# Expert weights of the second block read in rows of 1024 columns instead of halves of 512

## The chip, the cores and the metric

The kernel runs on one core of one Trainium2 chip. The metric is the device time of one execution in microseconds. It is the time of the whole kernel, two transformer blocks on 256 tokens of 1024 features, of which the change touches the mixture of experts in the second block.

## The reference

Everything is fp32. The second block has two layers; after each layer's mixer (a state-space mixer in layer 0, attention in layer 1) stands a mixture of 16 experts in which each expert picks its 32 best tokens of a sample. In layer 0 it runs on two samples, the latent tokens x and the context tokens; in layer 1 on x alone. All three matrices of an expert are 1024 x 1024:

```python
def moe_ec(h, router_w, w1, w3, w2):
    """Expert choice: each expert picks its top-C tokens of this sample's routed set."""
    b, T, _ = h.shape
    cap = EC_CAPACITY * T // N_EXPERTS_2
    logits = jnp.einsum('btd,de->bte', h, router_w, preferred_element_type=jnp.float32)
    aff = jax.nn.softmax(logits, axis=-1)
    gate, idx = lax.top_k(jnp.swapaxes(aff, 1, 2), cap)
    bidx = jnp.arange(b)[:, None, None]
    xg = h[bidx, idx]
    a = jnp.einsum('becd,edf->becf', xg, w1)
    g = jnp.einsum('becd,edf->becf', xg, w3)
    y = jnp.einsum('becf,efd->becd', jax.nn.silu(a) * g, w2)
    y = y * gate[..., None].astype(y.dtype)
    return jnp.zeros_like(h).at[bidx, idx].add(y.astype(h.dtype))
```

The result is the final rmsnorm of x after layer 1. The experts' weights are 2 x 16 x 3 matrices of 4.19 MB, 402.7 MB of the 597 MB that the kernel reads.

## The kernel before

The first block (mixer, attention over a memory, grouped experts) takes the first part of the time and isn't touched. In the second block, `choice` sets up a layer's experts, `choice_route` chooses the tokens and builds `xg`, the chosen rows turned to features (128 features on the partitions, 8 chunks k), and `choice_run` runs the experts in groups that fill 128 rows: layer 0 has 64 rows per expert (two samples of 32), so EG = 2 experts in each of 8 groups; layer 1 has 32 rows, so EG = 4 in each of 4 groups.

`choice_group` does one group. `product` (matmul at L1773) multiplies the group's rows with a matrix: the rows of expert j use their own S = 64 or 32 columns of TensorE (`tile_position=(0, j * S)`), so the experts of a group can run beside each other; the output is one PSUM bank, 128 x 512. For each half n of the hidden columns: w1's half into one bank, w3's half into another, tanh on ACT (L1804), two DVE operations that make silu(a) * g (L1805, L1806), four transposes on PE (L1809), a copy on ACT into `actT` (L1810). Then, for each half n of w2's columns: the product, scaled into `y` as a high and a low part (ACT L1815, DVE L1816); per sample and per 128 tokens two matmuls that put the rows back to their tokens (L1822), a product with the gate row on DVE (L1825) and the addition to x or ctx (L1826, on DVE for the first 128 tokens, on POOL for the others).

The weights come through a ring of slots of 16 KB per partition (`ring`, L110), 2.097 MB each: seven slots in layer 0 (the last opens when the routing's own pool closes), nine in layer 1. `choice_tile` (L1635) fills a slot by EG DMAs, one per expert, from SP's queue: the q-th part of the rows of EG experts, half n of the columns, that is 8 / EG chunks of 128 rows x 512 columns, so 2 KB of consecutive memory per row. Each layer has 96 such tiles. A slot is loaded again when PE has read its tile for the last time.

A scheduler sets the order of each engine's instructions from a simulated time; PE's first products of layer 0 and layer 1 stand among the last steps of the routing (L1741), which builds `xg` chunk by chunk. The final norm's gain row is loaded into `ctx_x[:, 0]`, the context's tile, which is free in layer 1 and serves as `actT` there (L2072 to L2075).

Of the kernel before, what the change touches and what calls it, by code (L numbers as in the profile page):

```python
# [22 lines left out]
AF = mybir.ActivationFunctionType  # L23
OP = mybir.AluOpType
AX = mybir.AxisListType
PSUM = bass.MemoryType.PSUM
DRAM = bass.MemoryType.DRAM

P = 128
# [49 lines left out]
class Net:  # L79
# [16 lines left out]
    @contextmanager  # L96
    def psum(self, **bufs):
        """PSUM's eight banks by the tags that a phase takes them under"""
        self.n += 1
        with self.tc.tile_pool(name=f"psum{self.n}", bufs=1, space=PSUM, reuse_waits="tile") as p:  # L100
            old = self.pp, self.pb
            self.pp, self.pb = p, bufs
            yield
            self.pp, self.pb = old
# [5 lines left out]
    def ring(self):  # L110
        """the next weight slot: the lasting ring and a phase's own in turn"""
# [7 lines left out]
        if hold is not None:  # L119
            # its load is not to come before what the phase at hand loads  # L120
            self.nc.gpsimd.tensor_copy(t[:, :1], hold)
# [3 lines left out]
    def weight_slots(self, n, side=None):  # L125
        """n more slots for weights, used in turn with those there are"""
# [38 lines left out]
    def columns(self, groups):  # L165
        """vectors over features, turned into one value per partition"""
# [31 lines left out]
    def load_more(self):  # L198
# [4 lines left out]
        # vectors laid out in every partition  # L203
# [25 lines left out]
    def rstd(self, ss, n, width):  # L229
        """(ss / width + EPS) ** -0.5 for [P, n]"""  # L230
# [16 lines left out]
    def norm_rows(self, xs, A4, rs=None):  # L247
        """rows scaled to unit mean square (no gain): one tile per 128 rows"""
# [13 lines left out]
    def norm_halves(self, xs, tile_, rs=None):  # L262
        """the same in tiles of 128 rows' halves; row tile i's chunk k"""
# [19 lines left out]
    def to_features(self, rows, g, hT, t0=0):  # L283
        """hT[:, k, t0:] = gain * transposed rows"""
# [17 lines left out]
    def rope(self, o, x, cg, sg, tmp, twice=None):  # L302
        """o = x * cg + swapped halves of x * sg; [P, 2, heads, d] with tables [P, 2, d]"""
# [14 lines left out]
    def twice(self, o, x, y, op):  # L318
        """o [P, 2, heads, 2, d]: x op y, twice"""
# [4 lines left out]
    def head_rms(self, x, sq, width):  # L324
        """x [P, 2, heads, width] scaled by its heads' rstd; sq a scratch of its shape"""
# [37 lines left out]
    def gained(self, g, d0, d, step, name):  # L363
        """tables of rope with the gain g of its dims in it"""
# [29 lines left out]
    def attend(self, PT, L, v_of, o_ps, shared):  # L394
        """o_ps [P = (parity, 64), heads / 2, P] from weights L [P, heads, nk]"""
# [70 lines left out]
    def chunks(self, *tiles):  # L466
        """of (hi, lo) tiles the list of their chunks' pairs"""
        return [(hi[:, k], lo[:, k]) for hi, lo in tiles for k in range(hi.shape[1])]

    def to_features_split(self, rows, g, hT):  # L470
        """gain * transposed rows, as a pair of which the sum is that"""
# [13 lines left out]
    def wpairs(self, how, pieces, K, c):  # L485
        """a weight in pairs of its K chunks of 128 rows: [P, 2, c] each"""
# [14 lines left out]
    def split_w(self, how, w):  # L501
        """a pair of a weight's chunks, split: for each chunk its hi and lo"""
# [10 lines left out]
    def lin3(self, how, w, hT):  # L513
        """rows of h times w: one PSUM tile per 128 rows"""
# [9 lines left out]
    def feat3(self, how, w, hT, done):  # L524
        """w^T h, feature-major, two chunks of 128 outputs per PSUM tile: done(chunk, psum)"""
# [11 lines left out]
    def mixer(self, keep, tile_, pool):  # L537
# [23 lines left out]
        # indexer  # L561
# [11 lines left out]
        # latent projections  # L573
# [8 lines left out]
        # queries of the attention over the chosen keys  # L582
# [56 lines left out]
        # gates: tanh of half the logits  # L639
# [8 lines left out]
        # the merge, feature-major: 2 * merged  # L648
# [37 lines left out]
    def index_mask(self, i, s):  # L686
        """0 for the 64 highest scores among the keys that a query sees, NEG for the others"""
# [9 lines left out]
    def latent_heads(self, h0, cT, kpe, tile_, M):  # L697
        """queries, keys (turned) and values of four heads"""
# [66 lines left out]
    def padded_keys(self, tile_, k, cT, sT, tag):  # L765
        """one key head, turned: kT[:, 0] has it in partitions 0:64, kT[:, 1] in 64:128"""
# [14 lines left out]
    def pairs_T(self, A4, q):  # L781
        """[P, 2, 2n heads, 64] -> [P = (parity, 64), n, T]"""
# [13 lines left out]
    def memory_keys(self, keep, M, G):  # L796
        """two pieces of work that wait for nothing: the memory's keys (turned) and values"""
# [43 lines left out]
    def memory_read(self, keep, pool):  # L841
# [3 lines left out]
        # queries, feature-major; the norm's gain is in their weights, its rstd with their own in the logits  # L845
# [76 lines left out]
    def raw_features(self, x, junk, put):  # L922
        """both 128 rows of x, turned: put(where, psum); the rstd of their norm"""
# [15 lines left out]
    CAP = 64  # L939

    def group_moe(self, pool, tile_, late):
# [20 lines left out]
        # group: softmax, first of the largest  # L962
# [19 lines left out]
        # experts of the group: the two largest of affinity + bias  # L982
# [22 lines left out]
        # place of a token in its expert's queue  # L1005
# [5 lines left out]
        # 1000 for a token that isn't there  # L1011
# [15 lines left out]
        # the context's rows will be normalised next  # L1027
# [9 lines left out]
    def group_weights(self, what):  # L1037
        """of a pair of experts half of the rows of gate and up, or all of down"""
# [15 lines left out]
    def down_half(self, late, pr, n):  # L1054
        """half of the columns of a pair of experts' down"""
# [6 lines left out]
    def group_round(self, r, ahead, tile_, late, hi, lo, pos, comb):  # L1062
        """tokens whose place in their expert's queue is in CAP * r + [0, CAP)"""
# [33 lines left out]
        for pr in range(E // 2):  # L1097
            if pr == 2:
                gather(1, "tf")
            # where the slots come from, and their weights  # L1100
# [81 lines left out]
    def ada_step(self, l, n=1):  # L1182
        """n 48ths of layer l's modulation: each from 128 of the features a sixth of its columns"""
# [51 lines left out]
    def mod_cols(self, l, which, r):  # L1235
        """per feature: norm_w * (1 + scale), shift"""
# [7 lines left out]
    def to_features_mod(self, rows, m, sh, hT, t0, tmp=None):  # L1244
        """hT[:, k, t0:] = m * transposed rows + sh; with tmp, hT is a pair of which the sum is that"""
# [22 lines left out]
    def split(self, hi, lo, x, eng=None):  # L1268
        """x = hi + lo, each in float32r"""
# [3 lines left out]
    def mm3(self, p, L, R, start, stop, **kw):  # L1273
        """p += L^T R of split operands (all but the product of the two small parts)"""
# [42 lines left out]
    def ssd_steps(self, tile_, tmp_, A4, hT):  # L1317
        """step sizes and the cumulative sums of the decays; directions and heads over the partitions"""
# [41 lines left out]
        # from here on each of a direction's heads in four of the partitions  # L1360
# [10 lines left out]
        for d in range(2):  # L1371
# [11 lines left out]
            # moving side: cumulative sums of a quarter of the heads  # L1383
# [13 lines left out]
            # stationary side  # L1397
# [13 lines left out]
            # weights of the context's tokens in the state it leaves  # L1411
# [10 lines left out]
            # sums from x's first (or last) token on  # L1422
# [13 lines left out]
    def ssd_project(self, g, pt_, xt_, hT):  # L1436
        """a group's four heads, B and C, all convolved, and the gate; feature-major"""
# [59 lines left out]
    def ssd_group(self, g, xs, BT, CT, zz, tile_, last=None):  # L1497
# [22 lines left out]
        for q in range(2):  # L1520
# [7 lines left out]
            for st in range(2):  # L1528
                M = tile_([P, 4, T], "M", 2)
                ex = []  # L1530
                # (direction, stationary variant, tile of the rows l, on the diagonal)
# [19 lines left out]
        # the context's final states, and what they give x's tokens  # L1551
# [37 lines left out]
    def ssd_out(self, q, tile_):  # L1589
        """the context's tokens (q = 0) or x's"""  # L1590
# [32 lines left out]
    def ssd_rstd(self):  # L1623
        """of the gated rows, from their squares' sums by partition"""
# [10 lines left out]
    def choice_tile(self, nm, l, e0, EG, q, n):  # L1635
        """the q-th part of EG experts' rows, half n of their columns: [P, EG, 8 / EG, 512]"""
        K = 8 // EG
        v = self.ring().rearrange("p (e k c) -> p e k c", e=EG, k=K)
        for e in range(EG):
            src = self.a[nm][l, e0 + e, q * K * P:(q + 1) * K * P, n * 512:(n + 1) * 512]  # L1640
# [3 lines left out]
    def choice(self, l, samples, pool):  # L1644
        """samples: (token rows, row of the modulation); what of the experts' work lasts"""
# [462 lines left out]
```

## Time and profile before

| | us |
|---|---|
| median of 3 runs | 2299.51 (2298.75 to 2302.57) |
| the profiled execution's span | 2296.6 |
| outside the span | 2.9 |
| PE busy | 1981.3 (86%) |
| DVE, ACT, POOL busy | 966.7, 637.2, 449.2 |
| share of the chain that is `DMA w<-in_moe_w_dram` | 21% of the span |
| HBM read | 597.05 MB, 262 GB/s over the span |

All times below are from one profiled execution, and they stand against its own span of 2296.6 us; the other 2.9 us of the median lie outside of it. A line such as L1773 is a line of the kernel; names of tiles are given without their numbers, so `w` is any weight tile and `ps` any PSUM bank. A share of the DMA engines near or over 1 means that all 16 have packets all the time.

### The profile page before, as it was taken

How to read it: one execution, taken by the hardware profiler on the slowest of the kernel's cores; microseconds unless marked ns; L12 is line 12 of the kernel's file. 1: busy time of each engine (PE TensorE's matmuls, PEld its weight loads, DVE VectorE, ACT ScalarE, POOL GpSimd, SP SyncE). 2: the span in 40 equal slices, each digit the busy share in tenths (PEclk: the TensorE clock that was granted, in tenths of full speed). 3: DMA queues.
4: the chain of work that ended last, by engine and by line, in shares of the span. 5: the costliest groups of instructions: out<-in, count | busy, mean ns of one | idle time of the engine just before them, and what ended most of it. 6: DMA issues, size and time to landing. Idle time of an engine off the chain costs nothing. (4 is left out here: it accounts for less than half of the span.)

```text
span 2296.6 us, 24819 instructions
## 1 busy us (share of the span) xinstructions
PE 1981.3 (86%) x9384; PEld 1019.8 (44%) x9384; DVE 966.7 (42%) x1675; ACT 637.2 (28%) x1174; POOL 449.2 (20%) x487
## 2 busy tenths in 40 slices
PE   8889878889999999898898888887988788888886
PEld 7667633366776677565332222222755311111111
DVE  6875532268776677665312222223675210100101
ACT  6454422254554455443100000002453000000000
POOL 4430110032242232511101011112652000000000
PEclk9999989989999999999999999999999799999999
DMA  7554849823332322474999999998349899999997
GB/s 235 186 189 142 286 143 346 287 79 111 120 117 95 110 83 84 150 245 174 363 386 387 386 386 387 387 387 331 149 165 329 299 386 387 386 387 387 387 387 280
DMA packets 339421, 603.53 MB, mean 263 GB/s; under 512 B 23611, under 2 KB 97118, under 8 KB 339294
## 3 DMA queue, kind: packets, MB, share of 16 engines
q1 hardware_dynamic: 339294, 601.86, 73.7%
q8 instruction: 76, 1.25, 0.2%
q14 instruction: 51, 0.42, 0.1%
HBM read 597.05 MB, written 4.75 MB: 262 GB/s over the span
## 5 line engine op out<-in xcount | busy, mean ns | idle before, releaser
L1773 PE MATMUL ps<-w,xg 128*64 128x512 f32 (+1 forms) x2048 | 506.1, 611 | 95.2 <-DMA w<-in_moe_w_dram 95.1
L1773 PEld LDWEIGHTS ps<-w,xg 128*64 128x64 f32 (+1 forms) x2048 | 128.1, 124 | 445.6 <-DMA w<-in_moe_w_dram 267.3
L1826 POOL TENSOR_TENSOR x<-x,o 128x512 f32<-128x512 f32 x24 | 39.2, 1635 | 695.1 <-DVE o L1825 695.1
L1276 PE MATMUL ps<-hT,ws 128*128 128x512 f32 x384 | 162.3, 423 | 4.1 <-DVE ada L1215 4.1
L1773 PE MATMUL ps<-w,ctx 128*32 128x512 f32 x512 | 139.5, 608 | 25.6 <-DMA w<-in_moe_w_dram 25.6
L1278 PE MATMUL ps<-hT,ws 128*128 128x512 f32 x384 | 156.1, 406 | 0.0
L1277 PE MATMUL ps<-hT,ws 128*128 128x512 f32 x384 | 155.8, 406 | 0.0
L1773 PE MATMUL ps<-w,actT 128*64 128x512 f32 x512 | 126.7, 599 | 10.7 <-DMA w<-in_moe_w_dram 9.8
L1805 DVE SCALAR_TENSOR_TENSOR act<-act,ps 128x512 f32<-128x512 f32 x24 | 16.5, 687 | 252.6 <-ACT act L1804 252.6
L1806 DVE TENSOR_TENSOR act<-act,ps 128x512 f32<-128x512 f32 x24 | 16.5, 688 | 250.4 <-PE ps L1773 249.7
L1816 DVE SCALAR_TENSOR_TENSOR y<-ps,s,y 128x512 fp32r<-128x512 f32 x24 | 18.0, 750 | 227.7 <-ACT y L1815 227.7
L1481 DVE SCALAR_TENSOR_TENSOR conv<-pad,cols,conv 128x512 f32<-128x512 f32 x124 | 103.6, 836 | 2.4 <-ACT conv L1474 0.2
L1815 ACT ACTIVATE y<-ps,s 128x512 fp32r<-128x512 f32 x24 | 16.5, 687 | 290.1 <-PE ps L1773 271.8
L1276 PEld LDWEIGHTS ps<-hT,ws 128*128 128x128 f32 x384 | 74.3, 193 | 24.5 <-DVE ada L1215 5.3
L1773 PEld LDWEIGHTS ps<-w,ctx 128*32 128x32 f32 x512 | 25.4, 109 | 130.4 <-DMA w<-in_moe_w_dram 102.2
L1278 PEld LDWEIGHTS ps<-hT,ws 128*128 128x128 f32 x384 | 73.9, 192 | 17.4 <-issue 0.4
L1277 PEld LDWEIGHTS ps<-hT,ws 128*128 128x128 f32 x384 | 74.0, 193 | 16.2 <-issue 0.4
L1804 ACT ACTIVATE act<-ps 128x512 f32<-128x512 f32 x24 | 14.3, 597 | 234.6 <-PE ps L1773 232.9
L1773 PEld LDWEIGHTS ps<-w,actT 128*64 128x64 f32 x512 | 37.6, 136 | 79.9 <-issue 61.9
L1271 DVE TENSOR_TENSOR ws<-wr,ws 128x1024 fp32r<-128x1024 f32 x48 | 61.8, 1290 | 26.2 <-ACT ws L1270 17.9
L1822 PE MATMUL ps<-y,back 128*128 128x512 f32 x160 | 58.2, 450 | 16.6 <-ACT y L1815 7.5
L1271 DVE TENSOR_TENSOR ws<-w,ws 128x1024 fp32r<-128x1024 f32 x46 | 61.3, 1338 | 21.8 <-ACT ws L1270 21.6
(632 smaller groups left out, 3754.3 us busy)
## 6 DMA issues: line engine op xcount, KB each, us to landing
w<-in_moe_w_dram SPq DMA_DIRECT2D x192, 1024.0 KB
w<-in_moe_w_dram SPq DMA_DIRECT2D x384, 512.0 KB
adaw<-in_ada_w_dram SPq DMA_DIRECT2D x34, 512.0 KB
w<-in_moe_w_up_dram SPq DMA_DIRECT2D x32, 512.0 KB
w<-in_moe_w_gate_dram SPq DMA_DIRECT2D x32, 512.0 KB
w<-in_moe_w_down_dram SPq DMA_DIRECT2D x16, 1024.0 KB
wr<-in_ssd_in_w_dram SPq DMA_DIRECT2D x16, 1024.0 KB
w<-in_ssd_out_w_dram SPq DMA_DIRECT2D x32, 512.0 KB
```

Of the source, the lines that this page charges most:

```text
L1271: (eng or self.nc.vector).tensor_tensor(lo, x, hi.bitcast(F32), op=OP.subtract)
L1276: t.matmul(p, lhsT=L[0], rhs=R[0], start=start, stop=False, **kw)
L1277: t.matmul(p, lhsT=L[0], rhs=R[1], start=False, stop=False, **kw)
L1278: t.matmul(p, lhsT=L[1], rhs=R[0], start=False, stop=stop, **kw)
L1481: nc.vector.scalar_tensor_tensor(seq(cv), pad[:, :, j:j + 256], tap(j), seq(cv), op0=OP.mult, op1=OP.add)
L1773: nc.tensor.matmul(p[j * S:(j + 1) * S], lhsT=x(k, j), rhs=w[:, j, kk], start=(k == 0), stop=(k == 7), tile_position=(0, j * S))
L1805: nc.vector.scalar_tensor_tensor(act, act, 1.0, pg[0], op0=OP.add, op1=OP.mult)
L1806: nc.vector.tensor_tensor(act, act, pg[1], op=OP.mult)
L1815: nc.scalar.activation(y[:, 0], p, AF.Copy, scale=ws)
L1816: nc.vector.scalar_tensor_tensor(y[:, 1], p, ws, y[:, 0].bitcast(F32), op0=OP.mult, op1=OP.subtract)
L1822: nc.tensor.matmul(q, lhsT=back[:, (2 * s + i) * P:(2 * s + i + 1) * P], rhs=y[:, v], start=(v == 0), stop=(v == 1))
L1826: (nc.gpsimd if i else nc.vector).tensor_tensor(xx[:, i, c], xx[:, i, c], o, op=OP.add)
```

## The change

A tile now holds whole rows: `choice_tile` loses the half n, takes 4 / EG chunks of 128 rows x 1024 columns, and its DMAs read 4 KB of consecutive memory per row. Slots, bytes, the number of tiles and of DMAs are the same. `product` takes two PSUM banks of one tag and fills both from each tile. The order of a group changes with it: w1 whole, tanh and the first DVE operation for both halves; w3 whole, the second DVE operation, transposes and copy for both halves; w2 whole, then both halves' y and return to the tokens. `actT` has one buffer instead of two; in layer 1 it is always `ctx_x[:, 0]` and the two `act` tiles are the halves of `ctx_x[:, 1]`.

```diff
-    def choice_tile(self, nm, l, e0, EG, q, n):
-        K = 8 // EG
+    def choice_tile(self, nm, l, e0, EG, q):
+        K = 4 // EG
...
-            src = self.a[nm][l, e0 + e, q * K * P:(q + 1) * K * P, n * 512:(n + 1) * 512]
+            src = self.a[nm][l, e0 + e, q * K * P:(q + 1) * K * P]
...
-            t = actT[:, grp % 2].rearrange("p (k c) -> p k c", k=8) if actT is not None else tile_([P, 8, P], "actT", 2)
-            self.choice_group(o["l"], grp, P // S, S, o["samples"], o["xg"], o["aff"], o["pos"], o["gr"], t, tile_)
+            if actT is None:
+                t, acts = tile_([P, 8, P], "actT", 1), [tile_([P, 512], "act", 2) for _ in range(2)]
+            else:
+                t, acts = actT[:, 0].rearrange("p (k c) -> p k c", k=8), [actT[:, 1, n * 512:(n + 1) * 512] for n in range(2)]
+            self.choice_group(o["l"], grp, P // S, S, o["samples"], o["xg"], o["aff"], o["pos"], o["gr"], t, acts, tile_)
...
-        e0, K = grp * EG, 8 // EG
-
-        def product(p, nm, n, x):
-            """p's rows by expert: x(k, expert) times the weights' half n"""
-            for q in range(EG):
-                w = self.choice_tile(nm, l, e0, EG, q, n)
+        e0, K = grp * EG, 4 // EG
+
+        def product(nm, x):
+
+            tag = self.turn("py")
+            ps = [self.ps(tag) for _ in range(2)]
+            for q in range(2 * EG):
+                w = self.choice_tile(nm, l, e0, EG, q)
                 for kk in range(K):
                     k = q * K + kk
-                    for j in range(EG):
-                        nc.tensor.matmul(p[j * S:(j + 1) * S], lhsT=x(k, j), rhs=w[:, j, kk],
-                                         start=(k == 0), stop=(k == 7), tile_position=(0, j * S))
...
+                    for n, p in enumerate(ps):
+                        for j in range(EG):
+                            nc.tensor.matmul(p[j * S:(j + 1) * S], lhsT=x(k, j), rhs=w[:, j, kk, n * 512:(n + 1) * 512],
+                                             start=(k == 0), stop=(k == 7), tile_position=(0, j * S))
+            return ps
...
-        junk = tile_([P, 512], "act", 1)[:, :nt * P]
+        junk = tile_([P, 512], "o", 2)[:, :nt * P]
...
-        for n in range(2):
-            pg, tag = [], self.turn("py")
-            for nm in ("moe_w1_2", "moe_w3_2"):
-                p = self.ps(tag)
-                product(p, nm, n, lambda k, j: xg[:, k, e0 + j].rearrange("p s c -> p (s c)"))
-                pg.append(p)
-            act = tile_([P, 512], "act", 1)
-            nc.scalar.activation(act, pg[0], AF.Tanh, scale=0.5)
-            nc.vector.scalar_tensor_tensor(act, act, 1.0, pg[0], op0=OP.add, op1=OP.mult)
-            nc.vector.tensor_tensor(act, act, pg[1], op=OP.mult)
+        rows = lambda k, j: xg[:, k, e0 + j].rearrange("p s c -> p (s c)")
+        for act, p in zip(acts, product("moe_w1_2", rows)):
+            nc.scalar.activation(act, p, AF.Tanh, scale=0.5)
+            nc.vector.scalar_tensor_tensor(act, act, 1.0, p, op0=OP.add, op1=OP.mult)
+        for n, p in enumerate(product("moe_w3_2", rows)):
+            act = acts[n]
+            nc.vector.tensor_tensor(act, act, p, op=OP.mult)
...
-        for n in range(2):
-            p = self.ps(self.turn("py"))
-            product(p, "moe_w2_2", n, lambda k, j: actT[:, k, j * S:(j + 1) * S])
+        for n, p in enumerate(product("moe_w2_2", lambda k, j: actT[:, k, j * S:(j + 1) * S])):
...
-                    o = tile_([P, 512], ("act", "o")[i], 1)
+                    o = tile_([P, 512], "o", 2)
```

The rest of the diff takes out comments, so the lines after it move by a few: the product's L1773 is L1779 in the changed kernel, L1822 is L1824, L2074 is L2076.

How the order of the engines moves is shown at three places. The first is PE where layer 0's experts begin, among the routing's steps: ps are PSUM banks, w2477, w2480 and the like the weight tiles in the ring, xg the chosen rows, L1741 the routing's products. Before:

```order
L1773 MATMUL ps2476_11429<-w2477_11430,xg_2215_10330 64x512 x2
L1773 MATMUL ps2479_11454<-w2480_11455,xg_2215_10330 64x512 x2
L1773 MATMUL ps2484_11487<-w2485_11488,xg_2215_10330 64x512 x2
L1741 MATMUL ps2464_11371<-oh_2460_11350,hi_2433_11251 128x512
L1741 MATMUL ps2464_11371<-oh_2460_11350,lo_2434_11252 128x512
...
L1773 MATMUL ps2476_11429<-w2477_11430,xg_2215_10330 64x512 x2
L1773 MATMUL ps2479_11454<-w2480_11455,xg_2215_10330 64x512 x2
L1773 MATMUL ps2484_11487<-w2485_11488,xg_2215_10330 64x512 x2
```

After:

```order
L1779 MATMUL ps2478_11431<-w2480_11433,xg_2215_10330 64x512 x2
L1779 MATMUL ps2479_11432<-w2480_11433,xg_2215_10330 64x512 x2
L1779 MATMUL ps2484_11483<-w2486_11485,xg_2215_10330 64x512 x2
L1779 MATMUL ps2485_11484<-w2486_11485,xg_2215_10330 64x512 x2
L1741 MATMUL ps2464_11371<-oh_2460_11350,hi_2433_11251 128x512
L1741 MATMUL ps2464_11371<-oh_2460_11350,lo_2434_11252 128x512
...
L1779 MATMUL ps2478_11431<-w2480_11433,xg_2215_10330 64x512 x2
L1779 MATMUL ps2479_11432<-w2480_11433,xg_2215_10330 64x512 x2
```

Before, three tiles are each read once in a step, and each holds four chunks. Now a step reads a tile into two banks, and the first tile, w2480, is read for the last time in the second step.

The second is PE at the end of layer 1 (each pair of return products stands twice, for y's two parts; the second pair is left out). ps3387 (before) and ps3369, ps3370 (after) are the banks of the last w2 product, y the scaled result, back the matrix that returns the rows to their tokens. Before:

```order
L1773 MATMUL ps3387_16483<-w3388_16484,ctx_3009 32x512 x6
L1773 MATMUL ps3387_16483<-w3389_16497,ctx_3009 32x512 x8
L1773 MATMUL ps3387_16483<-w3390_16510,ctx_3009 32x512 x8
L1773 MATMUL ps3387_16483<-w3391_16523,ctx_3009 32x512 x8
L1822 MATMUL ps3393_16539<-y_3392_16536,back_3352_16181 128x512
L1822 MATMUL ps3395_16545<-y_3392_16536,back_3352_16181 128x512
...
```

After:

```order
L1779 MATMUL ps3369_16407<-w3378_16500,ctx_3009 32x512
L1779 MATMUL ps3370_16408<-w3378_16500,ctx_3009 32x512
L1779 MATMUL ps3369_16407<-w3378_16500,ctx_3009 32x512
L1779 MATMUL ps3370_16408<-w3378_16500,ctx_3009 32x512
L1824 MATMUL ps3380_16516<-y_3379_16513,back_3346_16175 128x512
L1824 MATMUL ps3382_16522<-y_3379_16513,back_3346_16175 128x512
...
L1824 MATMUL ps3385_16531<-y_3384_16528,back_3346_16175 128x512
L1824 MATMUL ps3387_16537<-y_3384_16528,back_3346_16175 128x512
...
```

Before, the last four return products are those of the second half alone; now the last product feeds both halves in turn, one bank after the other on the columns of the same expert, and eight return products follow it.

The third is SP's queue in layer 1's last group, where w names a weight tile and ctx the context's. Before:

```order
L1641 DMA w3362_16276<-in_moe_w3_2_dram 128x2x512 x4
L1641 DMA w3366_16300<-in_moe_w1_2_dram 128x2x512 x4
L2074 DMA ctx_3009<-in_final_norm_w_2_dram 128x1024
L1641 DMA w3367_16313<-in_moe_w1_2_dram 128x2x512 x4
L1641 DMA w3368_16326<-in_moe_w1_2_dram 128x2x512 x4
L1641 DMA w3369_16339<-in_moe_w1_2_dram 128x2x512 x4
L1641 DMA w3371_16353<-in_moe_w3_2_dram 128x2x512 x4
L1641 DMA w3372_16366<-in_moe_w3_2_dram 128x2x512 x4
```

After:

```order
L1641 DMA w3376_16474<-in_moe_w2_2_dram 128x1024 x4
L1641 DMA w3377_16487<-in_moe_w2_2_dram 128x1024 x4
L1641 DMA w3378_16500<-in_moe_w2_2_dram 128x1024 x4
L2076 DMA ctx_3009<-in_final_norm_w_2_dram 128x1024
L2027 DMA out_0_dram<-x_72 128x1024 x2
```

The load of the final norm's gain (into ctx, the context's tile) stood among the weights of the last group, and now stands behind the last weight tile, ahead of the output.

## Rows read from the trace of the kernel before

**Rows 1.** The page: its first line.

```profile
span 2296.6 us, 24819 instructions
```

**Rows 2.** The chain of waits in order of time: start us, us, what.

```profile
2270.44 10.69 DMA w<-in_moe_w_dram
...
2289.19 1.28 DVE x L2024
```

**Rows 3.** Windows: stretch, us, busy of PE, PEld, DVE, ACT, POOL, PEclk, DMA share, GB/s.

```profile
270.00:275.00 5.00, 4.29 (x19) 2.29 (x20) 3.30 (x10) 2.92 (x10) 1.16 (x2) 0.74 1.09 348
...
340.00:345.00 5.00, 5.00 (x22) 1.59 (x18) 0.00 (x0) 0.00 (x0) 0.00 (x0) 1.00 1.03 405
...
1641.00:1650.00 9.00, 7.33 (x51) 5.27 (x50) 7.46 (x9) 6.01 (x10) 5.81 (x5) 1.00 1.02 416
1661.00:1668.00 7.00, 3.65 (x22) 2.84 (x20) 4.10 (x7) 3.05 (x6) 2.78 (x4) 1.00 1.03 420
1078.00:1094.00 16.00, 15.69 (x67) 5.92 (x65) 2.43 (x3) 2.33 (x3) 0.00 (x0) 1.00 0.10 30
...
1150.00:1550.00 400.00, 339.95 (x1399) 116.19 (x1397) 86.59 (x156) 27.89 (x50) 38.77 (x29) 0.99 1.05 387
...
1850.00:2280.00 430.00, 359.66 (x1325) 69.66 (x1318) 32.45 (x59) 14.72 (x28) 11.50 (x7) 1.00 1.04 385
```

**Rows 4.** PE's waits in 1850:2280, then pieces of its timeline (start, us, instructions).

```profile
PEld ps L1773 <- DMA w<-in_moe_w_dram: 278.6, 273, 2.9
...
1586.20 3.65 PE L1773 MATMUL ps<-w,actT 128*64 128x512 f32 x16
...
2281.17 1.90 PE L1773 MATMUL ps<-w,ctx 128*32 128x512 f32 x10 [0.27 <-DMA w<-in_moe_w_dram]
```

**Rows 5.** The page's part 6: DMA issues of the experts' weights, count and size.

```profile
w<-in_moe_w_dram SPq DMA_DIRECT2D x192, 1024.0 KB
w<-in_moe_w_dram SPq DMA_DIRECT2D x384, 512.0 KB
```

**Rows 6.** DMA view of 270:275, 1641:1650, 1150:1550: queue: packets, MB, share.

```profile
q1 hardware_dynamic: 1755, 1.74, 109.2%
...
q1 hardware_dynamic: 927, 3.73, 102.1%
...
q1 hardware_dynamic: 77741, 154.39, 104.4%
```

**Rows 7.** Timeline of PE and SP where each layer's experts start.

```profile
1083.89 2.79 PE L1773 MATMUL ps<-w,xg 128*64 128x512 f32 x12
...
1091.58 2.79 PE L1773 MATMUL ps<-w,xg 128*64 128x512 f32 x12
...
1092.70 6.85 SPq L1641 DMA_DIRECT2D w<-in_moe_w_dram  x6
...
1791.79 1.92 PE L1773 MATMUL ps<-w,xg 128*32 128x512 f32 x16
...
1794.77 1.92 PE L1773 MATMUL ps<-w,xg 128*32 128x512 f32 x16
...
1795.89 2.65 SPq L1641 DMA_DIRECT2D w<-in_moe_w_dram  x5
```

**Rows 8.** DVE's groups in 1590.5:1598 (layer 0's end): count, busy us, mean ns.

```profile
L1825 DVE TENSOR_TENSOR o<-ps,g 128x512 f32<-128x512 f32 x2 | 1.4, 686 | 0.0
...
L1826 DVE TENSOR_TENSOR ctx<-ctx,act 128x512 f32<-128x512 f32 x1 | 0.7, 681 | 0.0
```

**Rows 9.** DVE's groups in 2283.5:2287.2 (layer 1's end).

```profile
L1816 DVE SCALAR_TENSOR_TENSOR y<-ps,s,y 128x512 fp32r<-128x512 f32 x1 | 0.8, 751 | 17.5 <-ACT y L1815 17.5
```

**Rows 10.** Timeline of SP before the end.

```profile
2188.21 0.56 SPq L2074 DMA_DIRECT2D ctx<-in_final_norm_w_dram  x1
```

**Rows 11.** Between w3 and w2: DVE's product (page, part 5), PE's transposes (timeline).

```profile
L1806 DVE TENSOR_TENSOR act<-act,ps 128x512 f32<-128x512 f32 x24 | 16.5, 688 | 250.4 <-PE ps L1773 249.7
...
1306.83 0.66 PE L1809 MATMUL ps<-const,act 128*128 128x128 f32 x4 [0.58 <-DVE act L1806]
```

More of the change, by code (lines that the diff above doesn't have):

```diff
@@ L1759, in turn, with choice_group @@
         return tags[self.turns % len(tags)]
-    def choice_group(self, l, grp, EG, S, samples, xg, aff, pos, gr, actT, tile_):
+    def choice_group(self, l, grp, EG, S, samples, xg, aff, pos, gr, actT, acts, tile_):
         nc = self.nc
         NS = len(samples)
-        e0, K = grp * EG, 8 // EG
-        def product(p, nm, n, x):
-            for q in range(EG):
-                w = self.choice_tile(nm, l, e0, EG, q, n)
+        e0, K = grp * EG, 4 // EG
[4 more added lines that the diff above has]
+                w = self.choice_tile(nm, l, e0, EG, q)
                 for kk in range(K):
                     k = q * K + kk
-                    for j in range(EG):
-                        nc.tensor.matmul(p[j * S:(j + 1) * S], lhsT=x(k, j), rhs=w[:, j, kk],
-                                         start=(k == 0), stop=(k == 7), tile_position=(0, j * S))
+                    for n, p in enumerate(ps):
[3 more added lines that the diff above has]
+            return ps
         oc = tile_([P, NS, 2, EG, NS, 32], "oc", 1)
```

## Prediction

> **What bounds the kernel now.** I read the span and its chain of waits first, then the windows of the two stretches that load experts, then who waits for whom there. The profiled execution spans 2296.6 us [rows 1]; the median of the runs is 2299.51, so 2.9 us lie outside the span, and I leave them as they are. The chain that ended last is, in layer 1's experts, a ladder of transfers and nothing else: steps such as 10.69 us "DMA w<-in_moe_w_dram" follow each other to 2281.1 [rows 2]. Each step is two tiles of weights of 2.097 MB. The windows say the same of a whole stretch: from 1850 to 2280 the DMA share is 1.04 at 385 GB/s, and from 1150 to 1550 (layer 0's experts) 1.05 at 387 GB/s, while PE is busy 359.66 of 430 us and 339.95 of 400 us [rows 3]. PE's busy time is partly arrival: in the first of these stretches its weight loads wait 273 times for a transfer, 278.6 us in all [rows 4]. So both expert stages run at the pace of the DMA engines, and only what makes a byte arrive sooner, or what lies before the first and after the last transfer, moves the end.
>
> **Whole rows (half as many packets).** The change keeps the bytes and the number of DMAs (192 of 1024 KB and 384 of 512 KB [rows 5]) but each packet carries a row of 1024 columns, 4 KB, where it carried 2 KB. What a packet's length does is read from stretches of this trace in which the DMA engines are full: 1 KB packets (1755 packets, 1.74 MB) move at 348 GB/s, 2 KB packets (77741, 154.39 MB) at 387, 4 KB packets (927, 3.73 MB) at 416 [rows 3, 6]. Sixteen engines at those rates need 16 x 1024 / 348 = 47.1 ns for one 1 KB packet and 16 x 2048 / 387 = 84.7 ns for one of 2 KB. That is 37.6 ns per KB and a fixed 9.5 ns per packet; the same line gives 9.5 + 4 x 37.6 = 160 ns for 4 KB, an estimate of 410 GB/s. I take it, because the three short stretches with mostly 4 KB packets lie on both sides of it: 405 (340 to 345 us, with some shorter packets in it), 416 and 420 [rows 3]. A tile of 2.097 MB then takes 2.097 / 0.4096 = 5.120 us instead of 2.097 / 0.387 = 5.419, 0.299 us less. The bounds are 405 GB/s (5.178, 0.241 less) and 420 (4.993, 0.426 less).
>
> How many tiles run at that pace? Each layer has 96. In layer 0 six are issued before the stretch in which loading stops (see below) and 90 come after it: from SP's first issue at 1092.70 [rows 7] to the last tile's products at 1586.20 [rows 4] it is 493.5 us, 5.48 a tile with the first landing in it, so the stretch is full. In layer 1 eight are ahead and 88 behind. 178 x 0.299 = **-53.2 us** (bounds -42.9 and -75.8).
>
> The Trainium skill, "DMA: Bandwidth & Descriptors", section Specifications, asks for at least 512 B per transfer to reach line rate, and section "Where 436 GB/s comes from" says that for HBM to SBUF some 358 GB/s per core bind. By either, 2 KB rows would be as fast as 4 KB rows and this term would be nothing. The rows of this trace (348, 387 and 416 GB/s at 1, 2 and 4 KB) disagree with both, so I keep the term and give the rule a place among the rivals.
>
> **When loading starts again.** In both layers the ring is full while the tokens are routed, and transfers stop: from 1078 to 1094 the share is 0.10 [rows 3]. They resume when PE has read the first tile to its end. Before, a tile held four k-chunks of half the columns in layer 0, and PE's products come one chunk per 3.85 us there, at 1083.89 the second and at 1091.58 the fourth; SP issues again at 1092.70 [rows 7]. Now a tile holds two k-chunks of whole rows, and the order shows it read for the second time, and last, in the second step. Two steps are 7.7 us; that a step's products on one tile now follow each other on the same columns (two times 0.9 us) I take off, which leaves **-6 us**; 0 if another tile of the ring holds the queue, -7.7 at the most. In layer 1 a tile held two chunks, at 1791.79 and 1794.77, and SP issued at 1795.89; now it holds one: 2.98 us sooner, less 0.9 for a second product on the same columns: **-2.1 us** (0 to -3).
>
> **Ends of the two layers.** Before, the last group's first half of w2 was finished, normed and added while the second half was still loading. Now both halves end with the last tile, so the first half's epilogue is no longer covered and the other half's queues behind it on DVE. In layer 0 that is the y of 0.75 us, four gate products of 0.69 and two additions of 0.68 [rows 8]: 0.75 + 2.76 + 1.36 = 4.87, less 0.4 for what PE does meanwhile: **+4.5 us**. In layer 1, one sample: 0.75 + 2 x 0.69 + 0.68 = **+2.8 us** [rows 8, 9]. Bounds 0 (if it hides behind the attention's first loads) and 7.7 for both.
>
> **The rest, at nothing.** The final norm's load stood among the last weights, at 2188.21 [rows 10]; the tile that it fills now holds the last products' operand, so SP issues it after PE's last product, behind every weight, and only the output stands behind it. A quarter of a tile is 1.3 us; the row norm reads it at 2289.19, some 6 us after the last product ends [rows 2, 4], and by my sum 2.8 us later still. If that cover were gone it would cost at most 4 us. A few steps of the attention change places; I give that 0, plus or minus 6. The two-bank products use the same number of matmuls on the same columns: before, a tile was eight instructions, each two records, and it is now. The act product, the eight transposes and the copy between w3 and w2 now stand together once per group instead of half by half; PE stops there for about 3 us (a product of 0.69 twice, 0.66 of transposes, a copy of that size [rows 11]), 12 times. The ring, six to eight tiles of 5 us, covers it: transfers are queued over 30 us ahead.
>
> **The sum**: 2296.6 - 53.2 - 6 - 2.1 + 4.5 + 2.8 = 2242.6, and with 2.9 outside, **2245 us**, 2.4% less.
>
> **Rivals.** *Row length does nothing.* 2 KB packets would already be at the ceiling, as the page's rule has it. Left are the start and the ends: -8.1 + 7.3, thus 2299. For it: the 4 KB stretches are only 5 to 9 us long and read other tensors. Against it: three of them agree, and the 1 KB stretch is slower by as much as the line asks. Chance 0.05.
>
> *The gap between w3 and w2 reaches the transfers.* If slots come free late there, each of 12 groups costs the 3 us, 36 in all: 2281. For it: the boundary is concentrated now. Against it: PE is done well before the transfers (it waits 273 times), so the ring empties only into the queue. It decides if PE's delay exceeds the queue's length. Chance 0.09.
>
> *PE becomes the bound (slower).* The two halves of one expert's chunk follow each other on the same columns of PE; before, the experts alternated. A record takes about 0.46 us on its columns (16 records in 3.65 us on two column groups, 10 records in 1.90 us on four [rows 4]). If a blocked one held up the experts behind it, 16 records would go one after another: 7.3 us a tile against 5.42 now, +1.9 x 178 = +338 less the other terms: about 2630. It decides as soon as a tile costs PE more than 5.42 us, and takes gain from 5.13 on. Against it: the row of 10 in 1.90 us (in sequence it would be 4.6) holds, by the order of the code, two records of one expert ahead of the others', and the others started in spite of them. Chance 0.05.
>
> **How the numbers follow.** Forecast 0.80, row length 0.05, gap 0.09, PE 0.05, others 0.01. About 0.2%, 4.6 us, is what a measurement of this kernel can tell from no change. The rate's bounds move the forecast from 2255 to 2222, the start and the ends by -9 to +8, the attention by 6. The range is 2226 to 2272: the upper end goes into the gap's case half paid. Faster: 0.80 + 0.09 = 0.89; same: 0.05; slower: 0.05 + 0.01 = 0.06.
>
> **What would show it.** The expert windows at 405 to 420 GB/s with packets of 4 KB, some 98 thousand packets fewer in all, DMA steps of 10.2 us instead of 10.8 for two tiles. SP's first issue after layer 0's routing near 1086 and PE still waiting on transfers. The last addition 2.8 us further behind the last product. Wrong: GB/s stays at 387 (row length), PE's waits on transfers vanish (PE), or holes in the DMA share at each group (gap).

## The result, and the profile after

The changed kernel takes 2235.46 us in the median of four runs (2233.46 to 2243.27) against 2299.79 of the kernel before (2298.75 to 2302.57): a ratio of 0.9727 with a 95% interval of 0.9709 to 0.9745. The forecast was 2245 us, in a range of 2226 to 2272. It lies within the range, some 10 us below the forecast.

The page of the changed kernel, its first line, the row of GB/s in 40 slices of the span, and the count of packets:

```profile
span 2232.2 us, 24802 instructions
...
GB/s 239 187 196 136 308 112 346 283 111 114 119 118 117 101 94 49 110 232 211 327 409 409 409 409 409 409 409 325 190 160 303 310 409 409 409 409 409 409 409 288
DMA packets 241118, 603.53 MB, mean 270 GB/s; under 512 B 23612, under 2 KB 97119, under 8 KB 240991
```

The same last line of the kernel before:

```profile
DMA packets 339421, 603.53 MB, mean 263 GB/s; under 512 B 23611, under 2 KB 97118, under 8 KB 339294
```

The bytes are the same, and there are 98,303 packets fewer, half of the 196,608 rows of 2 KB that the experts' 402.7 MB were. Seven slices in a row, in each layer, stand at 409 GB/s: no slice shows a hole where a group of experts ends.

Windows of the two expert stages of the changed kernel (the columns of rows 3: stretch, us, busy of PE, PEld, DVE, ACT and POOL, PE's clock, DMA share, GB/s), to be read against the last two of [rows 3]:

```profile
1150.00:1500.00 350.00, 333.38 (x1278) 123.09 (x1275) 83.26 (x156) 26.12 (x47) 41.98 (x29) 1.00 1.03 409
1850.00:2150.00 300.00, 298.96 (x983) 85.11 (x980) 24.96 (x44) 10.53 (x21) 9.71 (x6) 1.00 1.03 409
```

The rate went from 387 and 385 to 409 GB/s, in both stages at a full DMA share. The chain of waits in order of time (start us, us, what) shows the same in its steps, each two tiles:

```profile
1782.71 10.22 DMA w<-in_moe_w_dram
...
2049.19 10.22 DMA w<-in_moe_w_dram
...
2101.40 74.07 PE ps L1779 x231
2176.95 38.53 PE ps L1779 x125
```

The step of 10.69 us in [rows 2] is the last of its ladder; most of the others before take 10.8 us (10.83 at 2227.11), so two tiles arrive 0.6 us sooner. In the last stretch the chain names PE. PE's busy share is 298.96 of 300 us here, where it was 84%. That looks like a new bound, and the run `half_of_the_loads` below shows that it isn't one. Nor have PE's waits for transfers vanished, which the prediction gave as the sign of that case: from 1850 to 2200 its weight loads wait 232 times (us in total, times, longest), for less than the 278.6 us of [rows 4] but nearly as often.

```profile
PEld ps L1779 <- DMA w<-in_moe_w_dram: 66.8, 232, 1.4
```

The time can be laid out by marks on PE's timeline and SP's. The first row of each pair is PE, the second SP; layer 0 first, with the routing's second step between, then layer 1:

```profile
1075.49 3.65 PE L1779 MATMUL ps<-w,xg 128*64 128x512 f32 x16
...
1080.22 1.94 PE L1779 MATMUL ps<-w,xg 128*64 128x512 f32 x8
...
1082.19 8.07 SPq L1641 DMA_DIRECT2D w<-in_moe_w_dram  x5
...
1756.32 1.92 PE L1779 MATMUL ps<-w,xg 128*32 128x512 f32 x16
...
1758.30 1.75 SPq L1641 DMA_DIRECT2D w<-in_moe_w_dram  x4
```

Before, layer 0's first products stood here:

```profile
1080.04 2.80 PE L1773 MATMUL ps<-w,xg 128*64 128x512 f32 x12
```

The ends of the two layers, PE's timeline of the changed kernel (last products of layer 0, the return to the tokens, the first transposes of the attention; then the last products of layer 1):

```profile
1549.43 2.31 PE L1779 MATMUL ps<-w,actT 128*64 128x512 f32 x6
1551.72 1.52 PE L1824 MATMUL ps<-y,back 128*128 128x512 f32 x4
...
1566.03 0.66 PE L1254 MATMUL ps<-const,a 128*128 128x128 f32 x2 [4.22 <-DVE s L244]
...
2198.73 17.60 PE L1779 MATMUL ps<-w,ctx 128*32 128x512 f32 x54
2216.31 0.73 PE L1824 MATMUL ps<-y,back 128*128 128x512 f32 x2
```

and that of the kernel before between the layers:

```profile
1586.20 3.65 PE L1773 MATMUL ps<-w,actT 128*64 128x512 f32 x16
...
1598.95 0.66 PE L1254 MATMUL ps<-const,a 128*128 128x128 f32 x2 [4.84 <-DVE s L244]
```

From these marks:

| stretch (profiled executions) | before | after | difference | forecast |
|---|---|---|---|---|
| start to layer 0's first product | 1080.0 | 1075.5 | -4.5 | 0 |
| to SP's first new load | 12.7 | 6.7 | -6.0 | -6 |
| to layer 0's last product | 497.2 | 469.5 | -27.6 | -26.9 |
| to the attention's first transposes | 9.1 | 14.3 | +5.2 | +4.5 |
| to layer 1's first product | 192.8 | 190.3 | -2.5 | 0 |
| to SP's first new load | 4.1 | 2.0 | -2.1 | -2.1 |
| to layer 1's last product | 487.2 | 458.0 | -29.2 | -26.3 |
| to the end | 13.5 | 15.9 | +2.3 | +2.8 |
| sum | 2296.6 | 2232.2 | -64.4 | -54.0 |

### The profile page after: what moved, and what is told of

It is laid out like the page before. It is cut to its first block, busy times and chain, and to the rows that moved or that the text cites. A ratio compares the mean times of both kernels' runs of the same rounds, so it can differ in the third digit from the quotient of the medians.

```text
span 2232.2 us, 24802 instructions
## 1 busy us (share of the span) xinstructions
PE 2047.0 (92%) x9363; PEld 1082.7 (49%) x9384; DVE 962.1 (43%) x1675; ACT 637.2 (29%) x1174; POOL 453.3 (20%) x487
## 5 line engine op out<-in xcount | busy, mean ns | idle before, releaser
L1779 PE MATMUL ps<-w,xg 128*64 128x512 f32 (+1 forms) x2048 | 541.5, 603 | 22.3 <-DMA w<-in_moe_w_dram 22.2
L1779 PEld LDWEIGHTS ps<-w,xg 128*64 128x64 f32 (+1 forms) x2048 | 166.1, 123 | 367.1 <-issue 267.2
L1779 PE MATMUL ps<-w,ctx 128*32 128x512 f32 x512 | 157.9, 598 | 0.5 <-DMA w<-in_moe_w_dram 0.5
L1779 PE MATMUL ps<-w,actT 128*64 128x512 f32 x512 | 134.3, 599 | 7.3 <-DMA w<-in_moe_w_dram 7.3
L1779 PEld LDWEIGHTS ps<-w,ctx 128*32 128x32 f32 x512 | 43.2, 109 | 110.1 <-issue 76.7
L1779 PEld LDWEIGHTS ps<-w,actT 128*64 128x64 f32 x512 | 45.5, 136 | 86.1 <-issue 63.4
L1277 PEld LDWEIGHTS ps<-hT,ws 128*128 128x128 f32 x384 | 74.0, 193 | 16.2 <-issue 0.4
L1827 DVE TENSOR_TENSOR o<-ps,g 128x512 f32<-128x512 f32 x80 | 51.7, 686 | 60.9 <-PE ps L1824 60.4
L1271 DVE TENSOR_TENSOR ws<-wr,ws 128x1024 fp32r<-128x1024 f32 x48 | 61.8, 1290 | 26.2 <-ACT ws L1270 17.9
L1542 POOL TENSOR_TENSOR seg<-seg,seg 128x512 f32<-128x512 f32 x32 | 44.9, 1403 | 124.3 <-ACT seg L1540 124.3
L1540 ACT ACTIVATE seg<-ps 128x512 f32<-128x512 f32 x96 | 55.3, 599 | 49.5 <-PE ps L1538 22.0
L1270 ACT ACTIVATE ws<-w 128x1024 fp32r<-128x1024 f32 x52 | 54.2, 1054 | 42.7 <-PE ps L1278 31.7
```

What stands on the lines that cost most here:

```text
L1270: self.nc.scalar.activation(hi, x, AF.Copy)
L1271: (eng or self.nc.vector).tensor_tensor(lo, x, hi.bitcast(F32), op=OP.subtract)
L1277: t.matmul(p, lhsT=L[0], rhs=R[1], start=False, stop=False, **kw)
L1540: nc.scalar.activation(e, p, AF.Exp)
L1542: nc.gpsimd.tensor_tensor(ex[0][0], ex[0][0], ex[1][0], op=OP.add)
L1779: nc.tensor.matmul(p[j * S:(j + 1) * S], lhsT=x(k, j), rhs=w[:, j, kk, n * 512:(n + 1) * 512], start=(k == 0), stop=(k == 7), tile_positio ...
```

## The experiments

**The packets' length by itself.** The changed kernel with its order, its banks and its ring, but each row of the weights put into two places of the tile, so that a packet is 2 KB again. (Layer 0's transfers are 512 KB instead of 1 MB, since one chunk goes with each. The product, left out here, reads each half from its new place.)

```diff
-        v = self.ring().rearrange("p (e k c) -> p e k c", e=EG, k=K)
+        v = self.ring().rearrange("p (n e k c) -> p n e k c", n=2, e=EG, k=K)
         for e in range(EG):
-            src = self.a[nm][l, e0 + e, q * K * P:(q + 1) * K * P]
-            self.nc.sync.dma_start(v[:, e], src.rearrange("(k p) c -> p k c", p=P))
+            for k in range(K):
+                src = self.a[nm][l, e0 + e, (q * K + k) * P:(q * K + k + 1) * P]
+                self.nc.sync.dma_start(v[:, :, e, k], src.rearrange("p (n c) -> p n c", n=2))
```

> The changed kernel with everything as it is (two banks, order, ring), except that each row of 1024 columns is put into two places of the tile, so a packet is 2 KB again instead of 4 KB. Theory (the length of the packets is the gain): the expert stages go back from 409 to about 387 GB/s, a tile from 5.13 to 5.42 us, 178 x 0.29 = 52 us: about 2288 us. Rival (the two-bank order is the gain): it stays near 2235 us.

Measured: 2293.36 us, a ratio to the kernel before of 0.9977 (0.9967 to 0.9987). Its windows:

```profile
1150.00:1500.00 350.00, 324.62 (x1217) 112.78 (x1214) 80.09 (x150) 25.45 (x47) 40.55 (x29) 1.00 1.05 386
1850.00:2150.00 300.00, 299.06 (x917) 79.93 (x915) 19.80 (x35) 9.17 (x17) 6.48 (x4) 1.00 1.05 387
```

The rate is back at 386 and 387 GB/s, and nearly all of the gain is gone. The two-bank order alone is worth about 4 us (2297.23 of the kernel before beside it, less 2293.36; 3 to 8 by the interval). Note PE: 299.06 of 300 us busy at the lower rate too.

The run settles two more questions. Its packets in the first stretch (DMA view: queue, packets, MB, share) are 2 KB long although both halves of a row are read by one transfer and stand side by side in memory:

```profile
q1 hardware_dynamic: 70065, 135.07, 104.5%
```

So it is the packet that counts, which is consecutive in memory and in the tile, and not the consecutive memory by itself. And layer 1's transfers are 512 KB at both rates, 387 here and 409 in the changed kernel, so the size of a transfer isn't the cause.

What the packets alone are worth in each layer can be read from its marks (SP's first new load and PE's last product, layer 0 and then layer 1):

```profile
1088.59 10.24 SPq L1642 DMA_DIRECT2D w<-in_moe_w_dram  x12
...
1581.46 3.65 PE L1780 MATMUL ps<-w,actT 128*64 128x512 f32 x12 [0.79 <-DMA w<-in_moe_w_dram]
...
1793.37 2.50 SPq L1642 DMA_DIRECT2D w<-in_moe_w_dram  x4
...
2235.81 41.83 PE L1780 MATMUL ps<-w,ctx 128*32 128x512 f32 x128
```

These stretches are 496.5 and 484.3 us, against 497.2 and 487.2 before and 469.5 and 458.0 in the changed kernel. From here to the changed kernel they give 53.2 us. The time itself is 5 us above the 2288 expected; the rest of the difference between the two executions stands ahead of layer 0 and in the attention.

**A series of lengths.** Three kernels that differ from each other in nothing but the packets and the places of their pieces in the tile. A tile holds two experts x two chunks, and one partition gets two consecutive rows, 2p and 2p + 1, of each block of 256; the features in xg and actT are permuted to match by strided columns, and a helper that is left out here permutes the modulation's columns in the routing. The pair of rows is then put down whole (8 KB), by row (4 KB), or in quarters of a row (1 KB).

```diff
...
+        v = self.ring().rearrange("p (e k c) -> p e k c", e=2, k=2)
+        for e in range(2):
+            src = self.a[nm][l, e0 + e, q * 2 * P:(q + 1) * 2 * P]
+            self.nc.sync.dma_start(v[:, e], src.rearrange("(p k) c -> p k c", k=2))
...
-                nc.tensor.transpose(t[:, k], act[:, k * P:(k + 1) * P], self.ident)
+                nc.tensor.transpose(t[:, k], act.rearrange("s (q p k) -> s q k p", q=2, k=2)[:, k // 2, k % 2], self.ident)
...
-                nc.tensor.matmul(p, lhsT=v[:, i, k * P:(k + 1) * P],
+                nc.tensor.matmul(p, lhsT=v[:, i].rearrange("s (q p k) -> s q k p", q=4, k=2)[:, k // 2, k % 2],
```

For 4 KB and 1 KB (m = 2 and 8) the tile is cut as `"p (m e c) -> p m e c"` and the source as `"(p k) (n c) -> p (k n) c"` with n = m / 2.

> Two consecutive rows of a weight matrix go to one partition, so a packet is 8 KB; the features of xg and actT are permuted to match, and a tile holds two experts x 2 chunks in both layers. If a packet costs a fixed 9.5 ns and 37.6 ns per KB, 8 KB take 310 ns, 422 GB/s, 4.97 us a tile: 178 x 0.16 = 28 us below the changed kernel, and layer 1's first slot opens one chunk (3 us) later: about 2210 us. Rival (4 KB packets are already at the ceiling): the rate stays at 409 GB/s and the time near 2238 us.

> The same tiles and the same order of products as pairs_8kb, but each row of 1024 columns in its own place, so packets of 4 KB. Theory: 409 GB/s as in the changed kernel, time near 2238 us. It also has only two experts in a tile of layer 1, on two column groups of TensorE instead of four; if the columns of TensorE set the pace, layer 1 is slower than in the changed kernel.

> The same tiles and order as pairs_8kb with rows in four places each, so packets of 1 KB. Theory: 348 GB/s as in the stretch of 1 KB packets before, 6.03 us a tile, 178 x 0.90 = 160 us above pairs_4kb: about 2398 us. Rival (the two-bank order is the gain): near 2238 us.

Measured: 8 KB 2220.1 us, ratio 0.9662 (0.9641 to 0.9682); 4 KB 2244.12 us, ratio 0.9767 (0.9747 to 0.9786); 1 KB 2411.49 us, one run. Windows of the three in the same two stretches, 8 KB first, then 4 KB, then 1 KB:

```profile
1150.00:1500.00 350.00, 339.50 (x1325) 127.75 (x1325) 87.61 (x163) 27.39 (x49) 45.28 (x31) 1.00 1.01 420
1850.00:2150.00 300.00, 267.71 (x1008) 73.86 (x1008) 23.01 (x40) 10.14 (x20) 8.37 (x6) 0.99 1.01 420
```

```profile
1150.00:1500.00 350.00, 334.27 (x1287) 124.77 (x1284) 82.76 (x155) 26.70 (x48) 41.65 (x29) 1.00 1.03 409
1850.00:2150.00 300.00, 265.81 (x980) 71.51 (x978) 26.31 (x45) 11.52 (x22) 9.74 (x6) 1.00 1.03 409
```

```profile
1150.00:1500.00 350.00, 312.14 (x1085) 108.74 (x1085) 72.30 (x138) 22.25 (x40) 36.23 (x26) 1.00 1.09 348
1850.00:2150.00 300.00, 251.25 (x951) 68.39 (x948) 26.45 (x62) 11.28 (x21) 6.48 (x4) 0.98 1.07 341
```

and the packets in the first stretch, the DMA view (queue: packets, MB, share), of 8 KB and then of 1 KB:

```profile
q1 hardware_dynamic: 20146, 146.73, 101.1%
```

```profile
q1 hardware_dynamic: 120674, 121.68, 109.0%
```

The rates are 348, 386, 409 and 420 GB/s for packets of 1, 2, 4 and 8 KB. The line drawn through 1 and 2 KB before any of this gave 410 for 4 KB and 422 for 8 KB. 4 KB were not the ceiling, and a kernel with 8 KB is faster than the changed one. (The 341 of the 1 KB kernel's second window is low because its transfers start again only at 1854.5 us, within the window; its later slices stand at 348.) Against each other, 8 KB take 24.0 us less than 4 KB, where 28 were expected, and 1 KB 167 us more, where 160 were.

The times came out 6 to 14 us above what I expected of each, and a part of that is these kernels' own. From SP's issue of the first expert tile to layer 0's first product 116.7 to 119.6 us pass in the three, against 112.0 to 114.0 in the other five, and their permutation stands in that stretch. In layer 1 SP's first new load comes 4.9 us after the first product instead of 2.0, since a tile holds two chunks again. The expectation counted that for 8 KB and not for the other two.

The 4 KB kernel has two experts in a tile of layer 1 instead of four, and there PE is busy 265.81 of 300 us instead of 298.96, at the same 409 GB/s. So PE's busy share moved by 11 points and the rate by nothing.

**TensorE's own pace.** The changed kernel with every second tile of a product left out of the loading; the product uses the tile before it twice.

```diff
-                w = self.choice_tile(nm, l, e0, EG, q)
+                w = self.choice_tile(nm, l, e0, EG, q) if q % 2 == 0 else w
```

> The changed kernel with every second weight tile of a product not loaded: the tile before it is used twice, so half of the experts' weights are left out and the transfers would need 2.56 us per tile's products. It shows TensorE's own pace. Theory (experts on other column groups run beside a pair on the same columns): a tile's 16 records take about 3.5 us in layer 0 (8 of 0.43 us on each of two groups) and between 2.6 and 3.5 us in layer 1; with the boundaries of 12 groups now open, 1930 to 2000 us. Rival (a blocked record holds up the others, 7.3 us a tile): no faster than 2235 us.

Measured: 1943.63 us, one run, inside the 1930 to 2000. Its window in layer 0, and PE's timeline within layer 1:

```profile
1150.00:1350.00 200.00, 200.00 (x846) 69.98 (x845) 52.91 (x104) 16.16 (x30) 26.66 (x19) 1.00 0.64 235
```

```profile
1872.95 32.54 PE L1779 MATMUL ps<-w,xg 128*32 128x512 f32 x224
```

In layer 0 the DMA engines idle a third of the time (share 0.64), so here PE sets the pace: 235 GB/s is a tile in 8.92 us, and each serves two tiles' products, 4.46 us for one, with everything that PE does at a group's boundaries. In layer 1, 224 records, 14 tiles' products, take 32.54 us, 2.32 us for one. Both lie under the 5.13 us that a tile takes to arrive at 409 GB/s, and under the 4.99 at 420. The expectation had 3.5 us for layer 0, without the boundaries that the 4.46 contain, and 2.6 to 3.5 for layer 1, which is faster. The third rival's 7.3 us is refuted: records of other experts run beside a pair that shares its columns.

**The ends.** The changed kernel, but the last group of each layer loads and multiplies w2 by halves of 512 columns, as before.

```diff
-        for n, p in enumerate(product("moe_w2_2", lambda k, j: actT[:, k, j * S:(j + 1) * S])):
...
+        for n, p in enumerate(halves() if grp == 16 * S // P - 1 else product("moe_w2_2", xa)):
```

(`halves` is the loop of the kernel before over n, each product before its epilogue; `xa` is the function that stood in the call.)

> The changed kernel, but in the last group of each layer w2 is loaded and multiplied by halves of 512 columns as before (2 KB packets for 16 tiles). Theory of the ends: the first half's epilogue is covered again, so the stretch from layer 1's last product to the end goes from 15.9 us back to 13.6 and the stretch between the layers gets 3 to 5 us shorter, while 16 tiles cost 0.29 us more each, 4.7 us: in sum within 3 us of 2235. If the ends were longer for another reason, they stay as they are and the time rises by 5 us.

Measured: 2233.17 us, ratio 0.9712 (0.9684 to 0.9739), not to be told from the changed kernel's by its time. The trace shows both terms. PE's timeline, the end of layer 0 and the end of layer 1:

```profile
1553.74 3.65 PE L1828 MATMUL ps<-w,actT 128*64 128x512 f32 x14
...
1566.67 0.66 PE L1254 MATMUL ps<-const,a 128*128 128x128 f32 x2 [4.84 <-DVE s L244]
...
2215.41 1.90 PE L1828 MATMUL ps<-w,ctx 128*32 128x512 f32 x10 [0.27 <-DMA w<-in_moe_w_dram]
2218.15 1.52 PE L1841 MATMUL ps<-y,back 128*128 128x512 f32 x4 [0.84 <-ACT y L1834]
```

From layer 0's last product to the attention 9.3 us (14.3 in the changed kernel, 9.1 before); from layer 1's last product, 2217.3, to the span's end of 2230.9 13.6 us (15.9 and 13.5). The stretches from SP's first new load to the last product are 471.6 and 459.8 us, 2.1 and 1.8 longer than in the changed kernel, where I expected 2.3 each from eight tiles. So the longer ends are the two-half epilogue, as the prediction put it, and 2 KB rows for the last tiles give back about as much as they take.

## Why the prediction was right

**The rate.** The step that carries the forecast, a line through the trace's own 1 and 2 KB stretches, gave 410 GB/s; 409 was measured in both stages, and the 2 KB control took it away. From the control to the changed kernel, which differ in the packets (and, in layer 0, in the size of a transfer), layer 0's stretch became 27.0 us shorter and layer 1's 26.2, where the forecast had 26.9 and 26.3.

**Layer 1 became 29.2 us shorter, 2.9 more than forecast**, the largest miss among the terms that the change touches, and the packets are not its cause: the control, with the old packets and the new order, already has the 2.9 us (484.3 for 487.2). Nor was the rate of 387 GB/s wrong for layer 1, though its row says 385 [rows 3]. That window ends after the transfers have begun to run out; cut in two, it shows 387 before:

```profile
1890.00:2270.00 380.00, 319.42 (x1164) 61.00 (x1161) 28.06 (x47) 13.43 (x26) 9.90 (x6) 1.00 1.05 387
2270.00:2280.00 10.00, 8.18 (x32) 1.58 (x32) 0.00 (x0) 0.00 (x0) 0.00 (x0) 1.00 0.83 307
```

About half of the 2.9 us is the final norm's load, which stood among the weights [rows 10] and now stands behind them. The DMA view of the stretch, the kernel before and then the control:

```profile
DMA packets 95906, 185.34 MB, mean 380 GB/s; under 512 B 5648, under 2 KB 5648, under 8 KB 95888
```

```profile
DMA packets 95760, 184.80 MB, mean 382 GB/s; under 512 B 5632, under 2 KB 5632, under 8 KB 95744
```

The difference of 0.54 MB at 387 GB/s is 1.4 us. I named that move and asked only what it costs at its new place, not what it frees at the old one. The rest stands at the stretch's two ends: in its first 50 us the control moves 18.47 MB against 18.22, and in its last 30 us 10.00 against 9.65, together 0.60 MB or about 1.5 us. So in the new order the transfers are full sooner and stay full until nearer to the last product, which the forecast did not have; why, no run takes apart. In layer 0 the same comparison gives 0.7 us (496.5 for 497.2), which is that stretch's whole miss.

**The start of loading** came as put: 12.7 to 6.7 us, -6.0 against -6, and 4.1 to 2.0, -2.1 against -2.1. Counted from layer 0's first product, SP's load at 1082.19 is the 1086 of the forecast.

**The ends** came within 0.7 us: +5.2 for layer 0 (forecast +4.5) and +2.3 for layer 1 (forecast +2.8). In layer 0 the attention then took 2.5 us less than before, which the forecast did not have (it allowed 6 us either way there). It does not hide the longer end: with the short end of `last_groups_w2_by_halves` the attention took 188.8 us, and end and attention together 198.1, where they took 204.6 in the changed kernel. On the chain of waits 1.8 of the 2.5 us stand where the router's weights wait behind layer 1's first expert tiles, before and after:

```profile
1735.31 6.79 DMA w<-in_moe_w_dram
1742.12 9.37 DMA wr<-in_moe_router_w_dram
```

```profile
1702.30 6.01 DMA w<-in_moe_w_dram
1708.32 8.36 DMA wr<-in_moe_router_w_dram
```

That is 16.2 us and 14.4 us; the control has 15.0 there. So the tiles that are issued ahead of the routing, which the forecast left out of its 178, are on the path too, for a small part.

**The final norm's load is hidden.** SP issues it after the last product, and DMA view and DVE's timeline show when it lands and when it is read. The first fence is the DMA view of 2216 to 2226 in slices of 0.25 us, busy tenths and GB/s:

```profile
DMA  0000085989934100000000000000000000000000
GB/s 0 0 0 0 0 131 98 344 311 442 410 131 180 49 0 0 0 0 0 0 0 0 0 0 0 0 0 0 0 0 0 0 0 0 0 0 0 0 0 0
```

```profile
2216.39 0.33 SPq L2076 DMA_DIRECT2D ctx<-in_final_norm_w_dram  x1
...
2224.79 1.28 DVE L2026 SCALAR_TENSOR_TENSOR x<-x,s,ctx 128x1024 f32<-128x1024 f32 x1 [0.74 <-POOL s L235]
```

The packets are done by about 2219.5, and DVE, which reads the gain at 2224.79, waits for POOL and not for the load.

**The program's start.** Of the 4.5 us before layer 0's first product, 2.7 are not the change's: SP issues the second block's first expert tile at 963.5 us against 966.2 before, and all that stands ahead of it is the same program. The other 1.8 lie between that issue and the first product, 112.0 us against 113.8; the control has 114.0, and two more kernels with the changed kernel's start 112.3 and 113.3, so whether they belong to the packets stays open. Without the 2.7 the two executions differ by 61.7 us, and the forecast's 54.0 lies 7.7 from it: 2.9 and 0.7 in the two expert stretches, 2.5 in the attention, 1.8 here, less 0.2 at the ends. The interval of the ratio, 0.9709 to 0.9745, is 59 to 67 us, so the forecast was too careful by some 5 us at the least, by several small terms and not by the one that carries it. (Of the 2.9 us that it adds for what lies outside the span, about 1.8 do in each execution whose time and span are both on record; the rest is spread between executions.)

**The rivals.** That row length does nothing is refuted by four lengths. That the gap between w3 and w2 reaches the transfers is refuted by the steps of 10.22 us and the even 409 GB/s in the slices. That PE becomes the bound is refuted by the 4.46 and 2.32 us and by its waits, which are still there.

## What to carry to other kernels

Where a stage keeps all DMA engines full, look at the bytes of a packet, consecutive in memory and in the tile, before anything else: find stretches of the same trace with other packet lengths, draw the line of time per packet through them, and read from it what longer rows would give. The same tile can often be loaded with longer consecutive runs, by whole rows or by giving a partition neighbouring rows and permuting the other operand to match. When a product is merged into a larger step, count the epilogue that loses its cover at the end, and the load that no longer stands in the full queue. Before a rate is read from a window, see that the transfers last to its end.

## What the runs showed that I had not expected

A packet's time is a straight line in its length over the four lengths measured: 47.1 ns for 1 KB, 84.9 (at 386 GB/s), 160.2 (at 409) and 312.1 (at 420), each on one of 16 engines, where 9.5 + 37.6 per KB gives 47.1, 84.7, 159.9 and 310.3. Followed to very long packets, its slope would be 16 x 1024 / 37.6 = 436 GB/s, an extrapolation. The Trainium skill, "DMA: Bandwidth & Descriptors", section Specifications, gives 435 GB/s as the fabric's ceiling, which this slope agrees with and no expert stretch here reaches; the same section's 512 B for line rate and 358 GB/s for HBM per core do not agree with the 348, 386, 409 and 420 GB/s of this one core.

A busy share of 99.7% is no sign of a bound. In layer 1 the share was 99.7% at 409 GB/s and at the control's 387 alike; with half the loads left out the same products took less than half the time. A likely reason, worked out and not tested: each expert's transfer of 512 KB brings four records, two for each half, on one set of columns, and at the prediction's 0.46 us a record they take 1.8 us one after another. A transfer comes every 1.28 us (0.524 MB at 409 GB/s), so the next expert's records begin on other columns before those have ended, and some record runs at nearly every moment while most of the columns may be idle.
